# Start-up of a two-layer trunk kernel: x by 256 columns, weights in three cuts, first scaled copies on VectorE

## The chip, the cores and the metric

The kernel runs on one core of one Trainium2 chip. The metric is the device time of one launch in microseconds (us); less is better. One core has TensorE (PE, matrix products; its weight loads are listed as PEld), VectorE (DVE), ScalarE (ACT), GpSimd (POOL) and SyncE (SP, which here issues most transfers). The engines run on their own and wait for each other through semaphores.

## The reference

Two layers (DEPTH = 2) over x of 256 tokens and 1024 columns, all in fp32. What the change touches is the very beginning of layer 0: the norm and the first part of the combined projection.

```python
def rms_norm(x, g):
    xf = x.astype(jnp.float32)
    y = xf * lax.rsqrt(jnp.mean(xf * xf, axis=-1, keepdims=True) + EPS)
    return (y * g.astype(jnp.float32)).astype(x.dtype)

u = rms_norm(h, g_mix_pre)
(gq, gk, gv, gg, ra_f, ra_b, aq, ak, av, gate_a, gate_b) = jnp.split(u @ w_in, offsets, axis=-1)
```

Behind it come gated linear attention, attention with rotary positions, a merge, an output projection, a SwiGLU network and a per-layer embedding, twice.

## The kernel before

Every product is made of three passes. A factor is split into a high part (rounded to the matmul's format, by ACT) and a low part (the remainder, by VectorE); TensorE adds high x high, high x low and low x high. Weights come in units of about 1 MB (class `Stream`): SP issues the load into one of two raw buffers (`rawp`), ACT casts the high part `wh`, VectorE subtracts to get the low part `wl`, TensorE reads both. A raw buffer is free for the next load when its low parts are made; `ws.load()` issues the next load, `ws.pieces()` gives the two halves of a unit (high, low, raw).

The first four units are rows of `w_in`: unit n has k-tiles 2n and 2n + 1 (128 rows each) of 1056 columns: the decay ranks and the queries. The 1056 columns go to TensorE in three blocks `RQ` of 288, 384 and 384 columns, for both halves (`hf`) of 128 tokens, so six accumulators `acc_0rq`.

In layer 0 the row scale of the norm is applied later, so TensorE need not wait for it. The left factor is x transposed, times the gain column. `turn` transposes a 128x128 block of x on TensorE into a PSUM bank (one bank for four k-tiles of one half), `high` makes the scaled high part from it on ACT, `rest` the scaled remainder on VectorE (`scalar_tensor_tensor`, PSUM times gain minus high). `gains` transposes the gain vector into the column `gcol`. `low` makes a weight's low part, `split_here` both parts of a weight.

The order of this phase is written out by hand. `on(e, ...)` chains the instructions of one engine (or of SP's transfers, "dma") in the order in which they are written. The generator `start` emits the work in portions: `yield n` hands back until n ticks have passed, and the matmul loops call `tick()` after each group. The first portion holds the transposes of k-tiles 0 to 3, the scaled copies and the splits of the first unit. Transposes of later k-tiles, the splits of the second unit, the squares for the norm, and the third unit follow in later portions.

Transfers before: x columns 0-511 of half 0 on SP, of half 1 on ACT's queue, then the small gain vector on ACT's queue; k-tiles 0 and 1 of the first unit as two transfers of 1056 columns (`FIRST`); the second unit in one transfer; x columns 512-1023 as two.

Warm-up matmuls on constant data (`warm_up`) run before x is there: `WARM = 6, 6, 3` means six of 128 columns, six of 512, and three of 512 after the first transposes.

The first unit's matmuls (`rq_first`) run k-tile by k-tile over all six accumulators; units 1 to 3 go through `rq_step`, one accumulator and unit at a time, in the order `STEPS_FIRST`.

Of the kernel before, what the change touches and what calls it, by code (L numbers as in the profile page):

```python
# [48 lines left out]
UNIT = 2112  # L49
RQ = ((0, 288), (288, 672), (672, 1056))  # L50

WARM = 6, 6, 3

FIRST = (0, 0, 1056), (1, 0, 1056)
C_GQ, C_GK, C_GV, C_GG, C_RA = 0, 512, 1024, 2048, 3072
C_AQ, C_AK, C_GA, C_GB = 3104, 4128, 4640, 5664

# [2 lines left out]
def trunk_kernel(ctx: ExitStack, tc: tile.TileContext, a: dict, out: bass.AP):  # L60
# [78 lines left out]
    def on(e, f, *args, **kw):  # L139

        with tc.issue_after(line[e].ins) if e in line else nullcontext():
            line[e] = f(*args, **kw)
# [6 lines left out]

    grow = mid()[0:8, 0:P]  # L150

    def load_x(hf, j, e="dma", q=nc.sync):
        c = slice(j * 512, (j + 1) * 512)
        on(e, q.dma_start, h[:, hf, c], a["x"][0, hf * P : (hf + 1) * P, c])

    load_x(0, 0)
    load_x(1, 0, "act", nc.scalar)
    on("act", nc.scalar.dma_start, grow, a["g_mix_pre"][0].rearrange("(k p) -> k p", p=P))


# [29 lines left out]
    def unit_rows(w, n, c0=0, c1=D, parts=None):  # L190

        if parts:

            return lambda t: [
                (t[:, k * (c1 - c0) + x : k * (c1 - c0) + y], w[(2 * n + k) * P : (2 * n + k + 1) * P, c0 + x : c0 + y])
                for k, x, y in parts
            ]
        return lambda t: [
            (
                t[:, : 2 * (c1 - c0)].rearrange("p (k c) -> p k c", k=2),  # L200
                w[n * 256 : (n + 1) * 256, c0:c1].rearrange("(k p) c -> p k c", p=P),
            )
        ]

    plan = []
    for l in range(DEPTH):
        w = a["w_in"][l]
        plan += [unit_rows(w, n, C_RA, C_RA + 1056, FIRST if l + n == 0 else None) for n in range(4)]
        for c0 in (C_AK, C_GQ, C_GK, C_GV, C_GV + 512, C_GG, C_GG + 512):
            plan += [unit(w, kh, c0) for kh in range(2)]  # L210
        by_block = lambda w, c: [unit(w, kh, c + j * 512) for j in range(2) for kh in range(2)]
        gates, merges = by_block(w, C_GA), by_block(a["w_o_gla"][l], 0)
        pair = [unit(w, kh, C_GB + j * 512) for kh in range(2) for j in range(2)]
        for x in GATES:
            plan.append(gates.pop(0) if x == "u" else merges.pop(0) if x == "m" else (pair, int(x)))
        plan += by_block(a["w_o_attn"][l], 0)
        plan += [unit(a["w_out"][l], kh, j * 512) for kh in range(2) for j in range(2)]
        if l == 0:
            plan += [unit_rows(a["w_ple_proj"][l], 0)]
        w = a["w_ffn_in"][l]  # L220
        blocks = [[unit_gate_up(w, kh, b) for kh in range(2)] for b in range(NBLK)]
        plan += blocks[0] + blocks[1]
        plains = [u for b in PLAIN for u in blocks[b]]
        pairs = [[unit(w, kh, c + b * 256) for kh in range(2) for c in (0, HIDDEN)] for b in PAIRS]
        outs = [unit_rows(a["w_ffn_out"][l], n) for n in OUT]
        for x in FFN.replace("p", ""):
            if x == "1":
                pair = pairs.pop(0)
            plan.append(plains.pop(0) if x == "u" else outs.pop(0) if x == "o" else (pair, int(x)))
        plan += outs  # L230
        plan += [unit(a["w_ple_gate"][l], kh, j * 512) for kh in range(2) for j in range(2)]
        if l + 1 < DEPTH:
            plan += [unit_rows(a["w_ple_proj"][l + 1], 0)]

    class Load:
# [5 lines left out]
        def start(self):  # L241
            if self.own:
                self.raw = self.own()
            else:
                self.raw = rawp.tile([P, UNIT], F32, tag="raw", name=nm("raw"))
            return self.make(self.raw)

    class Stream:
# [33 lines left out]
                self.lend = False  # L282
            return wp.tile([P, UNIT], F32R, tag=tag, name=nm("lent")).bitcast(F32)

        def load(self, between=lambda: None):

            self.room += 1
            self.start(between)

        def start(self, between=lambda: None):  # L290
            while self.loads and (self.lend or not self.loads[0].waits) and (self.loads[0].own or self.room):
                x = self.loads.pop(0)
                self.room -= not x.own
                moves = x.start()
                for dst, src in moves:
                    if self.open:
                        nc.sync.dma_start(dst, src)
                    else:
                        on("dma", nc.sync.dma_start, dst, src)
                    between()  # L300
                x.n = sum(math.prod(dst.shape[1:]) for dst, _ in moves)

        def put(self, x, parts=2):
# [476 lines left out]


    ws.load()
    ws.load()
    load_x(0, 1)
    load_x(1, 1)
    unit_a, unit_b = ws.pieces()
    warm = accp.tile([P, 512], F32, tag="acc", name="warm")
    gcol = small(8, "gcol", 1)
# [42 lines left out]
    def gains():  # L831

        ps = aux()
        on("pe", nc.tensor.transpose, ps[:, 0:8], grow, ident[0:8, 0:8])
        on("dve", nc.vector.tensor_copy, gcol, ps[:, 0:8])
# [4 lines left out]
    def split_here(hi, lo, src):  # L840
        on("act", nc.scalar.copy, hi, src)
        low(hi, lo, src)
# [11 lines left out]
    def high(hf, *ks):  # L854

        for k in ks:
            ps = banks[hf, k // 4][:, k % 4 * P : (k % 4 + 1) * P]
            on("act", nc.scalar.activation, uT.at(k, 1, hf * P, P)[0][:, 0, :], ps, AF.Copy, bias=0.0, scale=gcol[:, k : k + 1])

    def rest(hf, *ks):  # L860

        for k in ks:
            ps = banks[hf, k // 4][:, k % 4 * P : (k % 4 + 1) * P]
            hi, lo = (t[:, 0, :] for t in uT.at(k, 1, hf * P, P))
            on("dve", nc.vector.scalar_tensor_tensor, out=lo, in0=ps, scalar=gcol[:, k : k + 1],
               in1=hi.bitcast(F32), op0=ALU.mult, op1=ALU.subtract)

    def start():
        cut = lambda piece, c: [t[:, c] for t in piece]
        gains()  # L870
        for hf in range(2):
            turn(hf, 0)
        for hf in range(2):
            high(hf, 0)
        warm_up(WARM[2], True)
        turn(0, 1)
        turn(1, 1)
        turn(0, 2, 3)
        for c in RQ:
            on("act", nc.scalar.copy, *(t[:, slice(*c)] for t in unit_a[::2]))  # L880
        rest(0, 0)
        rest(1, 0)
        low(*cut(unit_a, slice(0, 288)))
        high(0, 1)
        high(1, 1)
        low(*cut(unit_a, slice(288, 1056)))
        on("act", nc.scalar.copy, unit_b[0], unit_b[2])
        rest(0, 1)
        rest(1, 1)
        high(0, 2, 3)  # L890
        low(*unit_b)
        rest(0, 2, 3)
        ws.load()
        unit_c, unit_d = ws.pieces()
        yield 2
        turn(1, 2, 3)
        high(1, 2, 3)
        rest(1, 2, 3)
        yield 4
        split_here(*unit_c)  # L900
        split_here(*unit_d)
        ws.load()
        for hf in range(2):
            square(hf, 0)
        yield 2
        turn(0, 4, 5, 6, 7)
        for hf in range(2):
            square_here(hf, 1)
            rstd(hf)
        scales()  # L910
        ropes_first.extend(rope_tables(0))
        high(0, 4, 5, 6, 7)
        rest(0, 4, 5, 6, 7)
        yield 1
        turn(1, 4, 5, 6, 7)
        high(1, 4, 5, 6, 7)
        rest(1, 4, 5, 6, 7)
        for piece in ws.pieces():
            split_here(*piece)
        ws.load()  # L920
        ws.open = True
        ws.fill()
# [53 lines left out]
    for l in range(DEPTH):  # L976
# [92 lines left out]
            passes(o[:, : c1 - c0], parts, u == 0, u == 3, u == 0)  # L1069
            tick()  # L1070

        def rq_first(os_):

            for k in range(2):
                for hf, ps in ((0, (0, 2)), (1, (0, 2)), (0, (1,)), (1, (1,))):
                    ah, al = uT.tok(k, hf)
                    for b, (c0, c1) in enumerate(RQ):
                        h, lo = (t[:, k * 1056 + c0 : k * 1056 + c1] for t in us[0])
                        for p in ps:
                            x, y = ((ah, h), (ah, lo), (al, h))[p]  # L1080
                            mm(os_[hf, b][:, : c1 - c0], x, y, k + p == 0, False)
                    tick()

        steps = [(int(x[0]), b, int(x[1])) for x in (STEPS if l else STEPS_FIRST) for b in range(3)]
# [1 line left out]
        for n, (hf, b, u) in enumerate(steps):  # L1086
            if u == len(us):
                us.append(ws.take())
            if (hf, b) not in o:
                o[hf, b] = acc()  # L1090
            if l + u:
                rq_step(o[hf, b], hf, b, u)
            elif (hf, b) == (1, 2):
                rq_first(o)
            if all(s[2] != u for s in steps[n + 1 :]):
                ws.done()
            if u == 3:
                put_q(hf, b, o[hf, b])
# [608 lines left out]
```

## Time and profile before

| | |
|---|---|
| median of 3 runs | 921.12 us (920.63 to 921.78) |
| the profiled execution | 920.53 us, of which 918.8 us span |
| first matmuls of the first unit without a pause | from 7.66 us on |
| transfers | 173.44 MB, mean 189 GB/s |

How to read the rows: times are microseconds from the start of the span unless marked ns. A row of a timeline gives start, length, engine, line and operation, what is written <- what is read, the shape, the count of merged instructions, and in brackets how long the engine had been idle before and who ended that. A row of the chain of waits gives start, length, engine, tile and line. Instructions that go through `on` carry line 142, the warm-ups and the first unit's matmuls line 105, those of the later units line 121. Matmuls overlap: the spacing of their starts is their price, their own length is longer.

### The profile page before, as it was taken

To read this page: it belongs to the slowest core of one execution; us is meant where nothing else is said; L and a number is where in the kernel's file an instruction comes from. 1 tells how busy PE (TensorE), PEld (TensorE's weight loads), DVE (VectorE), ACT (ScalarE), POOL (GpSimd) and SP (SyncE) were. 2 spreads that over 40 slices of the span, in tenths; PEclk is the share of its full clock that TensorE was granted. 3 is DMA by queue.
4 is the path that set the end of the run, shared out by engine and by line. 5 is a ranking of instruction groups with operands and counts; after the bars stand their busy time and mean duration, and the time that the engine had idled before them with its cause. 6 is when DMAs were issued, how large, how long until landed. Compare 5 with 4: busy or idle time off the path is not lost.

```text
span 918.8 us, 12423 instructions
## 1 busy us (share of the span) xinstructions
PE 909.9 (99%) x4673; PEld 776.1 (84%) x4673; DVE 785.2 (85%) x1004; ACT 583.1 (63%) x968; POOL 93.1 (10%) x149
## 2 busy tenths in 40 slices
PE   9999999999999999999999999999999999999996
PEld 8998888888888888888899988888888888888886
DVE  6988989987669998999779789798875799989984
ACT  6688767564567565567675677765644766565563
POOL 3700212310000000000114001100001000000000
PEclk9999999999999999999999999999999999999999
DMA  8664445657385655657576424454673856555361
GB/s 277 206 199 135 138 138 189 212 184 244 107 298 183 210 197 189 244 158 260 195 238 210 158 92 138 138 202 164 201 256 103 278 170 212 215 173 225 124 243 46
DMA packets 88679, 173.44 MB, mean 189 GB/s; under 512 B 3422, under 2 KB 26470, under 8 KB 88108
## 3 DMA queue, kind: packets, MB, share of 16 engines
q1 hardware_dynamic: 88316, 172.27, 55.1%
q8 instruction: 36, 0.59, 0.3%
q10 hardware_dynamic: 304, 0.40, 0.1%
q14 instruction: 23, 0.19, 0.1%
HBM read 169.50 MB, written 3.15 MB: 188 GB/s over the span
## 4 chain that ended last, share of the span: by engine, by line
PE 92%; DVE 4%; issue 1%; ACT 1%; POOL 1%; DMA 1%; POOLq 0%; DVEq 0%; SPq 0%; ACTq 0%
PE acc_1ffnin L121 11%; PE acc_0ffnin L121 11%; PE acc_0gate L121 7%; PE acc_1gate L121 7%; PE acc_1ffnin L105 7%; PE acc_0ffnin L105 6%; PE acc_1rq L121 3%; PE acc_0gqk L121 3%; PE acc_0wout L121 2%; PE acc_1gqk L121 2%; PE acc_0ple L121 2%; PE acc_1gg L121 2%; PE acc_0v L121 2%; PE acc_0merge L121 2%; PE acc_1merge L121 2%; PE acc_1ple L121 2%
## 5 line engine op out<-in xcount | busy, mean ns | idle before, releaser
L105 PE MATMUL acc_0ffnin<-wh_0ffnin,big_0ffnin 128*128 128x512 f32 x176 | 57.0, 393 | 0.1
L105 PE MATMUL acc_1ffnin<-wh_1ffnin,big_1ffnin 128*128 128x512 f32 x176 | 56.8, 392 | 0.0
L133 ACT CAST wh_1ffnin<-raw_1ffnin 128x1024 fp32r<-128x1024 f32 x38 | 38.5, 1049 | 27.1 <-DMA raw_1ffnin<-in_w_ffn_out_dram 8.6
L133 ACT CAST wh_0ffnin<-raw_0ffnin 128x1024 fp32r<-128x1024 f32 x38 | 38.2, 1048 | 24.9 <-PE acc_0ffnin L121 7.4
L133 DVE TENSOR_TENSOR wl_1ffnin<-raw_1ffnin,wh_1ffnin 128x1024 fp32r<-128x1024 f32 x38 | 45.0, 1223 | 8.8 <-ACT wh_1ffnin L133 8.7
L133 DVE TENSOR_TENSOR wl_0ffnin<-raw_0ffnin,wh_0ffnin 128x1024 fp32r<-128x1024 f32 x38 | 44.7, 1222 | 8.1 <-ACT wh_0ffnin L133 8.0
L121 PE MATMUL acc_0ffnin<-wh_0ffnin,big_0wout 128*128 128x512 f32 x168 | 42.5, 393 | 0.0
L121 PE MATMUL acc_1ffnin<-wh_1ffnin,big_1wout 128*128 128x512 f32 x168 | 42.5, 393 | 0.0
L105 PEld LDWEIGHTS acc_0ffnin<-wh_0ffnin,big_0ffnin 128*128 128x128 f32 x176 | 33.0, 188 | 7.2 <-DVE big_0ffnin L133 0.5
L105 PEld LDWEIGHTS acc_1ffnin<-wh_1ffnin,big_1ffnin 128*128 128x128 f32 x176 | 33.0, 188 | 6.7
L133 DVE TENSOR_TENSOR wl_1ffnin<-lent_1ffnin,wh_1ffnin 128x1024 fp32r<-128x1024 f32 x30 | 35.9, 1221 | 1.7 <-ACT wh_1ffnin L133 1.7
L133 DVE TENSOR_TENSOR wl_0ffnin<-lent_0ffnin,wh_0ffnin 128x1024 fp32r<-128x1024 f32 x30 | 35.9, 1221 | 1.7 <-ACT wh_0ffnin L133 1.7
L121 PEld LDWEIGHTS acc_1ffnin<-wh_1ffnin,big_1wout 128*128 128x128 f32 x168 | 31.1, 188 | 6.2
L121 PEld LDWEIGHTS acc_0ffnin<-wh_0ffnin,big_0wout 128*128 128x128 f32 x168 | 31.1, 188 | 6.2
L133 ACT CAST wh_1ffnin<-lent_1ffnin 128x1024 fp32r<-128x1024 f32 x30 | 30.7, 1052 | 7.3 <-PE acc_1ffnin L105 3.9
L133 ACT CAST wh_0ffnin<-lent_0ffnin 128x1024 fp32r<-128x1024 f32 x30 | 30.7, 1054 | 7.0 <-PE acc_0ffnin L105 3.9
L105 PE MATMUL acc_1ffnin<-wl_1ffnin,big_1ffnin 128*128 128x512 f32 x88 | 34.3, 390 | 0.0
L105 PE MATMUL acc_0ffnin<-wl_0ffnin,big_0ffnin 128*128 128x512 f32 x88 | 34.3, 390 | 0.0
L133 DVE TENSOR_TENSOR wl_0gate<-raw_0gate,wh_0gate 128x1024 fp32r<-128x1024 f32 x20 | 24.3, 1260 | 5.3 <-ACT wh_0gate L133 5.2
L133 ACT CAST wh_0gate<-raw_0gate 128x1024 fp32r<-128x1024 f32 x20 | 20.0, 1049 | 13.1 <-DMA raw_0gate<-in_w_o_attn_dram 6.3
L133 DVE TENSOR_TENSOR wl_1gate<-raw_1gate,wh_1gate 128x1024 fp32r<-128x1024 f32 x20 | 23.6, 1223 | 5.4 <-ACT wh_1gate L133 5.2
L133 ACT CAST wh_1gate<-raw_1gate 128x1024 fp32r<-128x1024 f32 x20 | 20.0, 1049 | 11.7 <-DMA raw_1gate<-in_w_o_attn_dram 5.7
(710 smaller groups left out, 2705.4 us busy)
## 6 DMA issues: line engine op xcount, KB each, us to landing
raw_0ffnin<-in_w_ffn_out_dram SPq DMA_DIRECT2D x11, 1024.0 KB, 5.6
raw_1ffnin<-in_w_ffn_out_dram SPq DMA_DIRECT2D x11, 1024.0 KB, 5.2
lent_0ffnin<-in_w_ffn_in_dram SPq DMA_DIRECT2D x6, 1024.0 KB, 7.7
lent_1ffnin<-in_w_ffn_in_dram SPq DMA_DIRECT2D x6, 1024.0 KB, 6.7
raw_0v<-in_w_in_dram SPq DMA_DIRECT2D x4, 1024.0 KB, 4.9
raw_0gate<-in_w_o_gla_dram SPq DMA_DIRECT2D x4, 1024.0 KB, 5.2
raw_0gate<-in_w_o_attn_dram SPq DMA_DIRECT2D x4, 1024.0 KB, 5.6
raw_0wout<-in_w_ffn_in_dram SPq DMA_DIRECT2D x8, 512.0 KB, 5.0
```

The costliest lines, as they stand in the source:

```text
L105: return nc.tensor.matmul(o, lhsT, rhs, start=start, stop=stop)
L121: nc.tensor.matmul(o, x, y, start=start and n == 0, stop=stop and n == len(seq) - 1, **kw)
L133: return nc.scalar.copy(hi, src), nc.vector.tensor_tensor(out=lo, in0=src, in1=hi.bitcast(F32), op=ALU.subtract)
```

## The change

The first transfers, all on SP: x columns 0-255 of all 256 tokens; k-tile 0 as 288 and 768 columns, k-tile 1 as 1056; x columns 256-511; the second unit as two transfers of 1056 columns; x columns 512-1023. ACT's queue keeps the gain vector alone. Warm-ups become six narrow and three wide, and two narrow after the transposes. The first scaled copies of k-tiles 0 and 1, four in all, move from ACT to VectorE (`high_here`). The transposes of k-tile 1 come right behind those of k-tile 0; k-tiles 2 and 3 are turned in later portions. The cast of k-tile 1's weights on ACT is cut into the three blocks, its low part into two. `rq_first` now does the first two units, each k-tile by k-tile; in k-tile 0 it goes block by block over both halves, otherwise half by half.

```diff
-WARM = 6, 6, 3
+WARM = 6, 3, 2
-FIRST = (0, 0, 1056), (1, 0, 1056)
+FIRST = ((0, 0, 288), (0, 288, 1056), (1, 0, 1056)), ((0, 0, 1056), (1, 0, 1056))
...
-    def load_x(hf, j, e="dma", q=nc.sync):
-        c = slice(j * 512, (j + 1) * 512)
-        on(e, q.dma_start, h[:, hf, c], a["x"][0, hf * P : (hf + 1) * P, c])
-    load_x(0, 0)
-    load_x(1, 0, "act", nc.scalar)
+    def load_x(c0, c1):
+        on("dma", nc.sync.dma_start, h[:, :, c0:c1], a["x"][0, :, c0:c1].rearrange("(s p) c -> p s c", p=P))
+    load_x(0, 256)
...
     ws.load()
+    load_x(256, 512)
     ws.load()
-    load_x(0, 1)
-    load_x(1, 1)
+    load_x(512, 1024)
...
+    def high_here(hf, k):
+        ps = banks[hf, k // 4][:, k % 4 * P : (k % 4 + 1) * P]
+        hi = uT.at(k, 1, hf * P, P)[0][:, 0, :]
+        on("dve", nc.vector.tensor_scalar, out=hi, in0=ps, scalar1=gcol[:, k : k + 1], scalar2=None, op0=ALU.mult)
...
     def start():
+        def split_cut(piece):
+            for c in RQ:
+                on("act", nc.scalar.copy, *(t[:, slice(*c)] for t in piece[::2]))
         gains()
-        for hf in range(2):
-            turn(hf, 0)
-        for hf in range(2):
-            high(hf, 0)
-        warm_up(WARM[2], True)
-        turn(0, 1)
-        turn(1, 1)
-        turn(0, 2, 3)
-        for c in RQ:
-            on("act", nc.scalar.copy, *(t[:, slice(*c)] for t in unit_a[::2]))
+        for k in range(2):
+            for hf in range(2):
+                turn(hf, k)
+        warm_up(WARM[2])
+        for hf in range(2):
+            high_here(hf, 0)
+        split_cut(unit_a)
         rest(0, 0)
         rest(1, 0)
         low(*cut(unit_a, slice(0, 288)))
-        high(0, 1)
-        high(1, 1)
+        for hf in range(2):
+            high_here(hf, 1)
         low(*cut(unit_a, slice(288, 1056)))
-        on("act", nc.scalar.copy, unit_b[0], unit_b[2])
+        split_cut(unit_b)
         rest(0, 1)
         rest(1, 1)
-        high(0, 2, 3)
-        low(*unit_b)
-        rest(0, 2, 3)
+        low(*cut(unit_b, slice(0, 288)))
+        low(*cut(unit_b, slice(288, 1056)))
         ws.load()
         unit_c, unit_d = ws.pieces()
-        yield 2
+        yield 5
+        turn(0, 2, 3)
+        high(0, 2, 3)
+        rest(0, 2, 3)
+        split_here(*unit_c)
+        yield 1
         turn(1, 2, 3)
         high(1, 2, 3)
         rest(1, 2, 3)
-        yield 4
-        split_here(*unit_c)
+        yield 2
         split_here(*unit_d)
         ws.load()
         for hf in range(2):
             square(hf, 0)
-        yield 2
+        yield 3
         turn(0, 4, 5, 6, 7)
...
-        def rq_first(os_):
+        def rq_first(os_, u):
+            both = (0, 1)
             for k in range(2):
-                for hf, ps in ((0, (0, 2)), (1, (0, 2)), (0, (1,)), (1, (1,))):
-                    ah, al = uT.tok(k, hf)
-                    for b, (c0, c1) in enumerate(RQ):
-                        h, lo = (t[:, k * 1056 + c0 : k * 1056 + c1] for t in us[0])
-                        for p in ps:
-                            x, y = ((ah, h), (ah, lo), (al, h))[p]
-                            mm(os_[hf, b][:, : c1 - c0], x, y, k + p == 0, False)
+                rows = [[(b, hf, p) for p in (0, 2) for hf in both] for b in range(3)] if u + k == 0 else [
+                    [(b, hf, p) for b in range(3) for p in (0, 2)] for hf in both
+                ]
+                for row in rows + [[(b, hf, 1) for b in range(3)] for hf in both]:
+                    for b, hf, p in row:
+                        ah, al = uT.tok(2 * u + k, hf)
+                        c0, c1 = RQ[b]
+                        h, lo = (t[:, k * 1056 + c0 : k * 1056 + c1] for t in us[u])
+                        x, y = ((ah, h), (ah, lo), (al, h))[p]
+                        args = os_[hf, b][:, : c1 - c0], x, y, u + k + p == 0, False
+                        if u + k == 0 and p != 1:
+                            on("pe", mm, *args)
+                        else:
+                            mm(*args)
                     tick()
...
-            if l + u:
+            if l or u > 1:
                 rq_step(o[hf, b], hf, b, u)
             elif (hf, b) == (1, 2):
-                rq_first(o)
+                rq_first(o, u)
```

More of the change, by code (lines that the diff above doesn't have):

```diff
@@ L207, in trunk_kernel @@
         w = a["w_in"][l]
-        plan += [unit_rows(w, n, C_RA, C_RA + 1056, FIRST if l + n == 0 else None) for n in range(4)]
+        plan += [unit_rows(w, n, C_RA, C_RA + 1056, FIRST[n] if l == 0 and n < 2 else None) for n in range(4)]
         for c0 in (C_AK, C_GQ, C_GK, C_GV, C_GV + 512, C_GG, C_GG + 512):
@@ L283, in lent, with load, start @@
             return wp.tile([P, UNIT], F32R, tag=tag, name=nm("lent")).bitcast(F32)
-        def load(self, between=lambda: None):
+        def load(self):
             self.room += 1
-            self.start(between)
-        def start(self, between=lambda: None):
+            self.start()
+        def start(self):
             while self.loads and (self.lend or not self.loads[0].waits) and (self.loads[0].own or self.room):
@@ L299, in start @@
                         on("dma", nc.sync.dma_start, dst, src)
-                    between()
                 x.n = sum(math.prod(dst.shape[1:]) for dst, _ in moves)
```

## The prediction

> **What bounds the kernel now.** I read the page first, then the chain of waits in order of time, then the timeline of each engine over the first 36 us.
>
> ```profile
> PE 909.9 (99%) x4673; PEld 776.1 (84%) x4673; DVE 785.2 (85%) x1004; ACT 583.1 (63%) x968; POOL 93.1 (10%) x149
> ...
> PE 92%; DVE 4%; issue 1%; ACT 1%; POOL 1%; DMA 1%; POOLq 0%; DVEq 0%; SPq 0%; ACTq 0%
> ```
>
> TensorE (PE) is busy 909.9 of 918.8 us and carries 92% of the chain. What the change can win is the time at the start in which TensorE does nothing useful; whatever it wins there survives only if no later unit of weights is missed. The chain of waits (start, length, what):
>
> ```profile
> 1.04 3.38 PE warm L105 x12
> 4.42 0.12 issue
> 4.54 0.86 PE aux_start L142 x3
> 5.40 1.28 PE warm L105 x3
> 6.68 0.47 PE aux_start L142 x4
> ...
> 7.26 0.36 DVE big_start L142
> 7.62 0.04 issue
> 7.66 2.51 PE acc_0rq L105 x14
> 10.18 0.22 PE aux_start L142 x2
> 10.39 3.08 PE acc_0rq L105 x19
> 13.48 0.44 PE aux_start L142 x4
> ...
> 32.02 5.23 PE acc_0kv L121 x23
> ```
>
> Until 7.66 us the chain is warm-up matmuls, transposes and one wait for VectorE (DVE). The first unit (36 matmuls, k-tiles 0 and 1; some records are missing) ends at 13.48. Nineteen of its matmuls take 3.08 us, so 0.162 us each. From 13.48 on TensorE has no gap in the first 36 us.
>
> The pace matters. Three 512-column warm-ups take 1.28 us, 0.427 each; 512-column matmuls later take 5.23/23 = 0.227. So until about 6.6 us TensorE runs at half pace, though the granted clock (the last column but two of this stage row) reads 1.00 there:
>
> ```profile
> 5.75:6.00 0.25, 0.25 (x2) 0.02 (x1) 0.00 (x0) 0.24 (x2) 0.00 (x0) 1.00 0.94 389
> ```
>
> At half pace a column costs 0.427/512 us: 288 columns 0.24 us, 384 columns 0.32. The four transposes from 6.68 (0.47 us for four, against 0.86 for three before) are already at full pace. I go by the spacing, not by the granted clock.
>
> **The change: transfers.** Bytes moved, per microsecond from 0 on (view of the transfers, first 40 us), and the landings of the first x:
>
> ```profile
> GB/s 0 23 260 411 372 384 418 406 411 380 282 31 144 384 427 290 181 350 363 350 174 125 220 397 383 12 4 127 401 403 113 35 170 406 401 53 0 16 59 209
> h<-in_x_dram ACTq DMA_DIRECT2D x1, 256.0 KB, 3.4
> h<-in_x_dram SPq DMA_DIRECT2D x1, 256.0 KB, 3.2
> 0.79 0.38 SPq L142 DMA_DIRECT2D h<-in_x_dram  x1
> 1.22 1.38 SPq L142 DMA_DIRECT2D raw_start<-in_w_in_dram  x3
> ```
>
> Summed, the row gives 283 kB by 3.0 us, 694 by 4.0, 1066 by 5.0, 1450 by 6.0, 1868 by 7.0. The 524 kB of x are through at 3.6 and land at 4.0 and 4.2 (issue 0.79 + 3.2, and 3.4 on ACT's queue): 0.4 to 0.6 us after the last byte; I take 0.45. The new order is 262 kB of x, 147 kB and 393 kB of k-tile 0, 541 kB of k-tile 1, x columns 256-511, k-tiles 2 and 3, the rest of x. On the same curve these land at 3.35, 3.8, 4.8, 6.2, 6.9, 8.2, 9.5 and 10.9. [...] SP issues eight transfers at 0.46 (1.38/3) instead of six, done by 4.5, and only the load of g_gla_out stands behind them; ACT issues one fewer. That costs nothing: the next load that SP issues waits for VectorE anyhow (10.82, below).
>
> **Warm-up and transposes.** [...] The gain column's transpose needs only its own small load, now alone on ACT's queue. Four transposes from 3.35 at about 0.21 us issue spacing: half 0 has both k-tiles at 4.25, half 1 at 4.5. The three wide warm-ups that stood on the chain at 5.40 (1.28) become two narrow ones of 0.21, under VectorE's copies.
>
> **First scaled copies on VectorE.** No such copy of 128x128 from PSUM on VectorE is in the trace; the nearest rows:
>
> ```profile
> 5.22 0.63 ACT L142 ACTIVATE big_start<-aux_start,gcol_start 128x128 fp32r<-128x128 f32 x2 [2.10 <-PE aux_start L142]
> 5.86 1.26 ACT L142 CAST wh_start<-raw_start 128x288 fp32r<-128x288 f32 x3
> ...
> 7.26 0.61 DVE L142 SCALAR_TENSOR_TENSOR big_start<-aux_start,gcol_start,big_start 128x128 fp32r<-128x128 f32 x2 [2.27 <-PE aux_start L142]
> 7.79 1.32 DVE L142 TENSOR_TENSOR wl_start<-raw_start,wh_start 128x288 fp32r<-128x288 f32 x2
> ...
> 9.54 1.25 DVE L142 TENSOR_TENSOR wl_start<-raw_start,wh_start 128x1056 fp32r<-128x1056 f32 x1
> ```
>
> Two remainders take 0.61, so 0.27 spacing and 0.34 length; I use the same for a scaled copy (bounds 0.17, the 128x8 copy that VectorE makes at 4.82, and 0.37, ACT's length).
>
> ```profile
> 4.82 0.17 DVE L142 COPY gcol_start<-aux_start 128x8 f32<-128x8 f32 x1 [3.23 <-PE aux_start L142]
> ```
>
> The remainder at 7.26 waited 2.27 us for transposes, although its own k-tile had been turned at 5.2: it waits for whatever was written to that bank before it. That's why I let the copies wait for both k-tiles. Copies run 4.35-4.95, remainders of k-tile 0 until 5.5. ACT is free to cast: 288 columns by 4.25, the two others by 5.3 and 5.75 (a third of the 1.26 row each, some 0.45).
>
> **TensorE in the new order.** First matmul at 4.75. The four of block 0 are paced by VectorE (copy, copy, remainder, remainder) to 5.8. Then two at 0.32 until about 6.5, and at full pace six of 384 columns at 0.17: 7.5. Six with the weights' low part, 0.97: 8.5 (VectorE has those low parts at 7.3: two more copies 0.54, low parts 1.32). Two transposes, 0.22: 8.7. Eighteen matmuls of k-tile 1 at 0.162 and two more transposes: 8.7 + 2.9 + 0.22 = 11.8. Before: 13.48. **Lead 1.7 us.**
>
> [...]
>
> **Does the lead hold?** The second unit needs its high part from ACT at 10.5 and 12.1 (casts of 1.03, half of the 2.05 row below, behind the scaled copies), TensorE reaches it at 11.8 and 14.7. The tight one is the third:
>
> ```profile
> 10.82 0.38 SPq L142 DMA_DIRECT2D raw_start<-in_w_in_dram  x1
> 16.74 2.05 ACT L142 CAST wh_start<-raw_start 128x1056 fp32r<-128x1056 f32 x2 [0.41 <-DMA raw_start<-in_w_in_dram]
> 17.86 2.43 DVE L142 TENSOR_TENSOR wl_start<-raw_start,wh_start 128x1056 fp32r<-128x1056 f32 x2
> 20.54 0.29 PE L121 MATMUL acc_0rq<-wl_start,big_start 128*128 128x288 f32 x1
> 21.19 0.29 PE L121 MATMUL acc_0rq<-wl_start,big_start 128*128 128x288 f32 x1
> ```
>
> Its second low part is ready at 20.29 and first read at 21.19: slack 0.9. VectorE is busy from 7.26 to 20.29 without a pause but 0.23: 12.8 us of work. The change adds four copies (4 x 0.27 = 1.1) and one cut more in a low part (1.32 for two against 1.25: 0.1), and starts at 4.35. I add 0.7 of pauses: VectorE waits for ACT, which casts k-tile 2 only after two scaled copies that wait for TensorE's transposes at 8.5. 4.35 + 12.8 + 1.2 + 0.7 = 19.1. TensorE would read at 21.19 - 1.7 = 19.5, so the lead just holds, with 0.4 to spare; beyond that each tenth on VectorE costs a tenth. The third unit's load goes out when the first unit's raw buffer is free, at about 9.1 instead of 10.82; with the 5.9 us from 10.82 to 16.74 it lands at 15.0, before ACT is through with its copies (near 15.9). ACT has four copies less (2 x 0.63 = 1.26) and one cast cut in three (1.26 for 1.07 in one piece).
>
> The sum goes against the profiled execution: 920.53 us with a span of 918.8, the rest outside the span and untouched. 920.53 - 1.7 = 918.8; the median of the runs shown is 921.12, 0.6 above that execution, so the forecast for it is **919.4**. The cover that can go: VectorE's margin of 0.4 (1.3 us of extra delay there would leave 0.8 of the 1.7).
>
> **Rivals.** [...]
> (b) VectorE's backlog: 2.0 us of pauses instead of 0.7, low parts of the third unit at 20.4, TensorE stalls 0.9: gain 0.8, 920.3. For it: 12.8 us without a pause. Against: the next load is freed earlier too.
> [...]
> [...]
> That the change doesn't do what it says: x lands at 4.2 as now. Then everything up to 8.5 moves by 0.85, and the gain is 0.9; it falls in with (b) at 920.2.
>
> **How the numbers follow.** Forecast 0.40, (a) 0.10, (b) with the late x 0.12, (c) 0.25, (d) 0.13. A measurement of this kernel can tell 0.2%, 1.84 us, from no change: faster means under 919.28, slower over 922.96. The forecast's own range is 918.8 to 920.0 (x landing 3.0 to 3.6, copies 0.17 to 0.37), and the bound at 919.28 lies in its middle: half of it, 0.20, is faster, half the same. Faster: 0.20 + 0.25 = 0.45. Same: 0.20 + 0.10 + 0.12 = 0.42. Slower: 0.13. The range 918.3 to 921.5 takes in (a), (b) and most of (c) and leaves out (d) and the far end of (c).
>
> **What would show it.** In the changed profile: first x-transposes near 3.4; VectorE's scaled copies near 4.4 with 0.27 spacing; first acc_0rq matmul near 4.75; 0.32 us between 384-column matmuls turning to 0.17 near 6.6; the last matmul of the first unit near 11.8; low parts of the third unit by 19.1 and read at 19.5. Wrong it is if half pace goes on beyond 7 us, if TensorE waits for VectorE at the third unit, or if x lands no earlier than 4.

## The result, and the profile after

The changed kernel takes 922.64 us (median of 17 runs, 921.63 to 923.93), the kernel before 920.90 beside it (17 runs, 920.12 to 921.78). The ratio is 1.0020, 95% interval 1.0013 to 1.0027: 1.7 us slower. The profiled execution took 922.96 us (span 921.2) against 920.53 (918.8) before.

The page's first rows, with the chain's shares by engine:

```profile
PE 911.5 (99%) x4669; PEld 778.3 (84%) x4669; DVE 786.2 (85%) x1009; ACT 581.4 (63%) x966; POOL 92.7 (10%) x149
...
PE 94%; DVE 2%; ACT 1%; DMA 1%; issue 1%; POOL 1%; SPq 0%; POOLq 0%; DVEq 0%; ACTq 0%
```

TensorE was busy 911.5 us instead of 909.9, although it has six wide warm-ups fewer and only two narrow ones more: of the 2.4 us of span, 1.6 is TensorE being busy longer, and 0.8 is idle time. So two things went wrong. The chain of waits of the changed kernel (start, length, what) shows both:

```profile
1.79 4.60 DMA raw_start<-in_w_in_dram
...
6.42 0.52 ACT wh_start L142
...
6.98 4.69 PE acc_0rq L105 x14
...
12.09 1.23 PE acc_0rq L105 x6
...
13.54 3.84 PE acc_0rq L105 x24
...
22.11 11.62 PE acc_0rq L121 x72
...
33.95 5.23 PE acc_0kv L121 x23
```

First, a transfer now opens the chain: k-tile 0's second piece, issued at 1.79, lands at 6.39, and TensorE goes on only at 6.98. Second, fourteen matmuls from there take 4.69 us, 0.335 each: half pace. Only near 12.1 to 13.5 does the spacing become 0.16 (3.84/24). The trace's own record of TensorE's clock has its first change, to full, at 12.54; in the kernel before it was at 6.58. The keys and values start at 33.95 instead of 32.02, 1.93 late. From 6.98 on TensorE doesn't pause in this stretch.

TensorE's timeline has the pause (last column: idle before, and who ended it):

```profile
3.58 1.11 PE L142 MATMUL aux_start<-ident,h 128*128 128x128 f32 x4 [0.23 <-DMA h<-in_x_dram]
4.49 0.42 PE L105 MATMUL warm<-seed 128*128 128x128 bf16 x2
5.01 1.30 PE L105 MATMUL acc_0rq<-wh_start,big_start 128*128 128x288 f32 x4
6.98 2.93 PE L105 MATMUL acc_0rq<-wh_start,big_start 128*128 128x384 f32 x8 [0.67 <-ACT wh_start L142]
```

VectorE's timeline, the first scaled copies and the third unit's low parts:

```profile
4.52 0.61 DVE L142 TENSOR_SCALAR big_start<-aux_start,gcol_start 128x128 fp32r<-128x128 f32 x2 [0.97 <-PE aux_start L142]
...
21.11 2.42 DVE L142 TENSOR_TENSOR wl_start<-raw_start,wh_start 128x1056 fp32r<-128x1056 f32 x2
```

And ScalarE's, its first casts and the third unit's:

```profile
3.92 0.43 ACT L142 CAST wh_start<-raw_start 128x288 fp32r<-128x288 f32 x1 [1.20 <-DMA raw_start<-in_w_in_dram]
6.42 0.92 ACT L142 CAST wh_start<-raw_start 128x384 fp32r<-128x384 f32 x2 [2.06 <-DMA raw_start<-in_w_in_dram]
...
19.87 2.10 ACT L142 CAST wh_start<-raw_start 128x1056 fp32r<-128x1056 f32 x2
```

ACT sat idle 2.06 us for the second piece. VectorE's copies came as forecast, 4.52 and a spacing of 0.27 (0.61 for two). The third unit's cast, at 16.74 before, is at 19.87. It costs nothing here, because TensorE at half pace is late too. The third unit's load itself (its issue, then its landing in the view of the transfers) took 7.9 us, so it landed near 18.0; before, it was 5.9 us from issue to cast.

```profile
10.11 0.38 SPq L142 DMA_DIRECT2D raw_start<-in_w_in_dram  x1
...
raw_start<-in_w_in_dram SPq DMA_DIRECT2D x1, 1056.0 KB, 7.9
```

The view of the transfers, first 40 us: bytes moved per microsecond, and landings of the two pieces (the last column is the time from issue):

```profile
GB/s 0 17 284 189 326 358 320 324 403 415 392 338 227 351 326 203 121 88 161 401 406 329 135 14 53 207 408 377 23 129 399 414 96 45 227 403 365 16 0 0
...
raw_start<-in_w_in_dram SPq DMA_DIRECT2D x1, 384.0 KB, 4.6
...
raw_start<-in_w_in_dram SPq DMA_DIRECT2D x1, 144.0 KB, 2.6
```

Up to 3 us it moved as much as before (301 against 283 kB). From 3 to 4 it moved 189 instead of 411. The view by stages gives the next four microseconds (window, its length, granted clock, share of time that the DMA engines are busy, GB/s), first before:

```profile
4.00:8.00 4.00, 1.00 1.01 395
```

then after:

```profile
4.00:8.00 4.00, 1.00 0.99 332
```

The DMA engines are as busy and move 16% less. By 8.0 us 0.45 MB are missing (1.82 MB of 2.27).

### The profile page after: what moved, and what is told of

Read it like the earlier page. It is cut to its first block, busy times and chain, and to the rows that moved or that the text cites. A ratio compares the mean times of both kernels' runs of the same rounds, so it can differ in the third digit from the quotient of the medians.

```text
span 921.2 us, 12422 instructions
## 1 busy us (share of the span) xinstructions
PE 911.5 (99%) x4669; PEld 778.3 (84%) x4669; DVE 786.2 (85%) x1009; ACT 581.4 (63%) x966; POOL 92.7 (10%) x149
## 4 chain that ended last, share of the span: by engine, by line
PE 94%; DVE 2%; ACT 1%; DMA 1%; issue 1%; POOL 1%; SPq 0%; POOLq 0%; DVEq 0%; ACTq 0%
PE acc_0ffnin L121 12%; PE acc_1ffnin L121 11%; PE acc_1gate L121 7%; PE acc_0gate L121 7%; PE acc_0ffnin L105 7%; PE acc_1ffnin L105 7%; PE acc_1rq L121 3%; PE acc_0gqk L121 2%; PE acc_0wout L121 2%; PE acc_1gqk L121 2%; PE acc_0ple L121 2%; PE acc_1gg L121 2%; PE acc_0v L121 2%; PE acc_1merge L121 2%; PE acc_0merge L121 2%; PE acc_1ple L121 2%
## 5 line engine op out<-in xcount | busy, mean ns | idle before, releaser
L133 ACT CAST wh_1gate<-raw_1gate 128x1024 fp32r<-128x1024 f32 x20 | 20.1, 1050 | 12.1 <-DMA raw_1gate<-in_w_o_attn_dram 5.7
```

The source lines that it names most:

```text
L133: return nc.scalar.copy(hi, src), nc.vector.tensor_tensor(out=lo, in0=src, in1=hi.bitcast(F32), op=ALU.subtract)
```

## The experiments

Two theories from here on. CLOCK: a pause on TensorE ahead of full pace puts full pace off (in after a pause of 0.67 us ended at 6.98, and the clock was up at 12.54; in before the longest was 0.12, and it was up at 6.58); fewer warm-ups and the wait for the second piece make such pauses. TRANSFERS: the cut of k-tile 0 on SP's queue slows the first transfers, so that its second piece and the third unit are late. "Clock up" below is the first change in the trace's clock record, the spacing of matmuls agrees with it. "Reached" is the start of the first keys-and-values matmuls' stretch in the chain, 32.02 before and 33.95 after. The last four columns are of one profiled execution each, the median is of all runs.

| kernel | median us (lowest to highest) | before beside it | ratio, 95% | clock up | k-tile 0 complete | GB/s 4 to 8 us | reached |
|---|---|---|---|---|---|---|---|
| before (profile) | | | | 6.58 | | 395 | 32.02 |
| after (profile) | 922.64 (921.63–923.93) | 920.90 | 1.0013–1.0027 | 12.54 | 6.39 | 332 | 33.95 |
| e10, after again | 921.92, one run | 920.78 | | 7.85 | 6.07 | 284 | 32.75 |
| e1, after, filled | 922.00 (921.05–922.51) | 920.79 | 1.0002–1.0019 | 4.72 | 6.77 | 310 | 33.12 |
| e8, after, warm-ups of before | 921.46 (920.44–923.09) | 920.78 | 0.9996–1.0013 | 5.14 | 6.47 | 327 | 32.78 |
| e3, after, k-tile 0 whole | 921.67 (919.69–922.82) | 920.79 | 1.0001–1.0018 | 9.94 | 5.84 | 377 | 32.97 |
| e6, e3 filled | 921.34 (920.08–922.81) | 920.70 | 0.9996–1.0013 | 6.84 | 5.30 | 375 | 31.52 |
| e4, after, second piece on ACT's queue | 921.89 (921.47–925.09) | 920.79 | 1.0007–1.0026 | 10.46 | 5.3 | 382 | 32.80 |
| e5, e4 filled | 920.89 (919.38–922.89) | 920.70 | 0.9993–1.0010 | 5.50 | 5.4 | 395 | 30.95 |
| e12, e4 filled densely | 920.79 (919.63–922.31) | 920.66 | 0.9990–1.0009 | 5.87 | 5.4 | 352 | 30.93 |
| e7, after, loads and warm-ups of before | 920.63 (919.80–921.52) | 920.70 | 0.9991–1.0008 | 3.90 | 6.02 | 409 | 31.57 |
| e9, x on ACT's queue | 923.08 (922.12–924.46) | 920.78 | 1.0013–1.0034 | 9.87 | 5.12 | 395 | 33.45 |
| e2, before, fewer warm-ups | 921.90 (920.95–923.00) | 920.79 | 1.0000–1.0018 | 8.47 | | 379 | 32.54 |
| e11, before, k-tile 0 cut | 921.03 (920.29–922.46) | 920.66 | 0.9995–1.0013 | 5.23 | 6.97 | 332 | 32.67 |

### Fill TensorE's pauses (e1)

```diff
-WARM = 6, 3, 2
+WARM = 6, 4, 1
-        warm_up(WARM[2])
+        warm_up(WARM[2], True)
...
+                    if u + k + b == 0 and p == 2:
+                        for _ in range(2):
+                            on("pe", mm, os_[1, 2], seed, keep, True, True)
```

Two matmuls on constants go behind the fourth matmul; the accumulator that they write starts anew later.

> The changed kernel with its pauses on TensorE filled: one wide warm-up more before x, one wide in place of two narrow after the transposes, and two 512-column matmuls on constant data (into an accumulator that is cleared afterwards) between the first four and the fifth matmul. Theory CLOCK (the change lost because a pause of 0.67 us before the fifth matmul put full pace off from 6.6 to 12.5 us): full pace by 7.9 us at the latest, first unit done by 13.0 instead of 17.0 or so for the same work, time 919.8 to 920.6, 2 us below the changed kernel. Theory TRANSFER (the loss is the wait for the weights and the waits of ACT and VectorE behind it): the pause only holds other work, time 922.4 to 923.0 as the changed kernel.

The clock came up at 4.72, as CLOCK asks, and the median was 922.0 all the same, between the range that CLOCK gave and the one of TRANSFERS. The time went to another place; TensorE at the third unit in this run:

```profile
20.31 0.53 PE L121 MATMUL acc_0rq<-wh_start,big_start 128*128 128x288 f32 x2 [0.30 <-ACT wh_start L142]
21.28 0.89 PE L121 MATMUL acc_0rq<-wh_start,big_start 128*128 128x288 f32 x4 [0.44 <-ACT wh_start L142]
```

and the chain there:

```profile
2.25 6.12 DMA raw_start<-in_w_in_dram
...
9.69 0.97 DVE wl_start L142
...
10.68 8.48 DMA raw_start<-in_w_in_dram
...
19.18 0.88 ACT wh_start L142
...
20.16 1.07 ACT wh_start L142
...
21.28 11.63 PE acc_0rq L121 x70
```

The chain never touches TensorE before 21.28: k-tile 1's landing at 8.37 sets when the raw buffer comes free, hence the third unit's load at 10.68, which needs 8.5 us (before: 5.9 from issue to cast). A clock nearly 8 us earlier than in the profile of after won 0.83 us at the keys and values (33.95 to 33.12). The two costs stand in for each other: whoever removes one meets the other.

### Fewer warm-ups alone, in the kernel before (e2)

```diff
-WARM = 6, 6, 3
+WARM = 6, 3, 3
```

> The kernel before with three wide warm-ups fewer at the start, nothing else. They end at 3.1 instead of 4.4 us, x lands at 4.0 to 4.2: a pause of about 1 us. [...] Theory TRANSFER: 920.7 to 921.0, no change, because the warm-ups stand in a wait for x.

```profile
4.45 0.24 PE L142 MATMUL aux_start<-ident,mid_start 8*128 8x8 f32 x1 [1.30 <-DMA mid_start<-in_g_mix_pre_dram]
```

That is TensorE's timeline of e2: three warm-ups less leave a pause of 1.30 us; the clock comes up at 8.47 and the median rises by 1.1 us (the interval just touches no difference). In the profile of before they cover that wait, and the clock is up at 6.58.

### K-tile 0 whole again (e3), and whole and filled (e6)

```diff
-FIRST = ((0, 0, 288), (0, 288, 1056), (1, 0, 1056)), ((0, 0, 1056), (1, 0, 1056))
+FIRST = ((0, 0, 1056), (1, 0, 1056)), ((0, 0, 1056), (1, 0, 1056))
```

e6 has `WARM = 6, 4, 4` besides, the last four wide.

> The changed kernel with k-tile 0 as one transfer of 1056 columns again. If the cut made the transfer slow (third transfer starts at 245 GB/s and less between 3 and 4.2 us): k-tile 0 lands near 5.2 as a whole, first matmul at 5.7, no pause after it. Theory CLOCK: a pause from 4.7 to 5.7 in place of two of 0.35 and 0.67, dense from 5.7 on; full pace between 7 and 9.1, time 920.0 to 921.5. Theory TRANSFER: the weights arrive 1.2 us earlier, time 921.3 to 921.6, at whatever pace.

> k-tile 0 in one transfer as in the third experiment, TensorE kept busy until the first matmul (one wide warm-up more before x, four wide after the transposes). The third had its first matmul at 6.34 and half pace until 9.94. Theory CLOCK AND TRANSFER: full pace by 7.9 us, first matmul at 6.4, first unit done near 12.4, 919.8 to 920.5. Rival SUPPLY: 920.7 to 921.4, with a wait at the third unit. If CLOCK is no cause: 921.7 as the third.

The view by stages of e3:

```profile
4.00:8.00 4.00, 1.00 1.01 377
```

The whole k-tile of 528 KB is there at 5.84, before the last 384 KB of the cut one (6.39), and the rate is back. But TensorE now waits for its first matmul, and the clock comes at 9.94. Its timeline:

```profile
6.34 3.81 PE L105 MATMUL acc_0rq<-wh_start,big_start 128*128 128x288 f32 x12 [1.04 <-ACT wh_start L142]
```

Its median, 921.67, is above both ranges expected. With the pauses filled (e6) the clock is at 6.84 and the keys and values are reached 0.50 us ahead of before; its median is nevertheless 0.6 above before, an interval that includes no difference, and above the 919.8 to 920.5 of CLOCK AND TRANSFER. It lies in the range of the rival SUPPLY, but the wait at the third unit that this rival asks for isn't in the profile.

### The second piece on ACT's queue (e4), and filled (e5, e12)

```diff
-                for dst, src in moves:
-                    if self.open:
+                for i, (dst, src) in enumerate(moves):
+                    if i == 1 and len(moves) == 3:
+                        on("act", nc.scalar.dma_start, dst, src)
+                    elif self.open:
...
```

e5 has `WARM = 6, 4, 3` and e12 `WARM = 6, 5, 2` besides, the last ones wide.

> The changed kernel with the 768-column transfer of k-tile 0 issued by ACT instead of SP, so issued 0.5 us earlier and on the other queue. If the late landing (6.4 us) comes from the start of each small transfer behind the one before on a single queue: it lands near 5.2, the pause before the fifth matmul is gone. Theory CLOCK: full pace by 8 us in most runs, 920.0 to 921.0. Theory TRANSFER: 1.2 us less than the changed kernel, 921.4. If it still lands after 6, both expect 922.4 to 923.

> The 768 columns on ACT's queue as in the fourth experiment, and TensorE kept busy until the first matmul: one wide warm-up more before x, three wide in place of two narrow after the transposes. The fourth experiment began its first unit at 5.58 us but ran at half pace until 10.46. Theory CLOCK AND TRANSFER (both were needed): full pace by 7.9 us at the latest, first matmul at 5.8, first unit done near 12, 919.3 to 920.0, so 0.8 to 1.5 below the kernel before. Rival SUPPLY (the third unit's load, landing after 18 us, is the next bound, as in the first experiment where TensorE waited for its cast at 20.3 and 21.3): full pace early, but a wait of 1 us and more at the third unit, 920.5 to 921.3. If CLOCK is no cause: 921.9 as the fourth.

> The variant of the fifth experiment (768 columns on ACT's queue, TensorE kept busy) with one wide warm-up moved from behind the transposes to ahead of them: six narrow, five wide, two wide. [...] Theory CLOCK: full pace by 7.9 us in every execution, the slow executions (921.5 to 922.9) go, median 919.8 to 920.5 against 920.9. If the spread of the fifth had another cause (transfers): median and spread as there.

With the same cut on two queues the rate is 382 and both pieces are there at 5.3, the second 1.1 sooner than in after; but the first, which now shares the time with it, lands at 5.07 (3.8 us after its issue). So TensorE's timeline of e4 has its pause before the first matmul:

```profile
5.58 3.89 PE L105 MATMUL acc_0rq<-wh_start,big_start 128*128 128x288 f32 x12 [0.70 <-ACT wh_start L142]
```

With this one pause full pace came at 10.46 only: the pause has moved, not gone, and the median misses both theories' figures. e5 fills it, and its chain runs over TensorE alone from the transposes on:

```profile
0.79 3.23 DMA h<-in_x_dram
...
4.07 1.11 PE aux_start L142 x4
5.18 0.87 PE warm L105 x3
6.05 2.99 PE acc_0rq L105 x18
...
19.04 11.69 PE acc_0rq L121 x72
```

Eighteen matmuls take 2.99 us (0.166 each), the third unit is read from 19.04 on without a wait, and this execution took 919.45 us: it keeps its lead of 1.07 at the keys and values to the end. This is the course that the prediction described, some 1 us later and with the transfers split over two queues. Its twelve executions spread over 3.5 us, though, and their median of 920.89 is no better than before. e12, with one warm-up moved ahead of the transposes, reaches the keys and values 1.09 ahead too; in its profile most of that is lost at the start of layer 1, where TensorE waits in its timeline:

```profile
471.63 1.32 PE L446 MATMUL aux_0ple<-ident,mid_0ple 128*128 128x128 f32 x8 [0.40 <-DVE mid_0ple L516]
```

The profile of before has no such wait there. At the first keys and values of layer 1 0.35 of e12's lead is left (494.54 against 494.89). Its chain of waits there comes over a load of weights, ACT and VectorE, and reaches TensorE late:

```profile
459.55 6.39 DMA raw_0ple<-in_w_in_dram
...
472.63 2.43 DVE wl_1emb L133 x2
...
475.71 6.33 PE acc_1rq L121 x38
```

The chain of e6 does the same (a load of 6.04 us from 460.85 on, TensorE only from 476.67); e6, already 0.17 behind before at 444.55, is 0.61 behind at 495.50. In the profiles of before and e5 the chain stays on TensorE there. The spread of e12, expected to be narrower, stayed at 2.7 us, its median missed the 919.8 to 920.5 of CLOCK, and why some executions lose the lead later is open.

The medians, each less that of the before beside it, say the same: after +1.7; with the clock alone mended (e1, and e8 below) +1.2 and +0.7; with the transfers alone mended (e3, e4) +0.9 and +1.1; with both (e5, e12) +0.2 and +0.1, and +0.6 in e6.

### The new order with the loads of before (e7); the warm-ups of before with the new loads (e8)

e7 takes `FIRST`, `load_x` and its calls from before, and `WARM = 6, 6, 3`; e8 only `WARM = 6, 6, 3`. In both the last three are wide.

> The changed order of the work (copies on VectorE, two units k-tile by k-tile, later transposes) with the transfers and warm-ups of the kernel before (x by 512 columns on two queues, k-tiles 0 and 1 and the second unit uncut, six narrow, six wide, three wide). Only transfers and warm-ups are undone. If the loss came from these alone: full pace near 6.6, first matmul near 6.8 without the wait for remainders at 7.3, 920.0 to 920.8, at or below the kernel before. If the new order itself costs (VectorE's 1.2 us of extra work, ACT waiting for late transposes): 921.3 to 922.

> The changed kernel with the warm-ups of the kernel before (six narrow, six wide, three wide), nothing else undone. The transposes then start at 4.4 instead of 3.6 us and the first matmul at 6.6 instead of 5.0, but TensorE has hardly a pause. Theory CLOCK: full pace by 7.9 at the latest, first unit done near 13, 921.0 to 921.8, about 1.2 below the changed kernel, though its first matmul is 1.6 us later. If CLOCK is no cause, the later start only costs: 923 to 924.

e7 equals before (ratio 1.0000) and reaches the keys and values 0.45 us ahead, with a clock that in this profile came up 2.7 us earlier (3.90): the copies on VectorE and the k-tile order of two units cost nothing, and gain no more than that. e8 differs from e7 in the loads alone, and is 1.2 us behind it there; in its view by stages and on TensorE:

```profile
4.00:8.00 4.00, 1.00 0.95 327
```

```profile
19.98 0.53 PE L121 MATMUL acc_0rq<-wh_start,big_start 128*128 128x288 f32 x2 [0.27 <-ACT wh_start L142]
20.95 0.88 PE L121 MATMUL acc_0rq<-wh_start,big_start 128*128 128x288 f32 x4 [0.44 <-ACT wh_start L142]
```

The new loads, with a clock at 5.14, give the wait at the third unit again. The median, 921.46, is in CLOCK's range.

### X on ACT's queue (e9)

```diff
-    load_x(0, 256)
+    load_x(0, 256, "act", nc.scalar)
```

K-tile 0 whole on SP, `WARM = 6, 6, 1` with the last one wide.

> The changed kernel with the first 256 columns of x on ACT's queue beside k-tile 0 in one piece on SP's, and warm-ups six narrow, six wide, one wide. Both transfers are issued at 0.8 us. If a small transfer alone on a queue was what let the weights come late: k-tile 0 lands at 4.8 to 5.2 instead of 6.4, x at 4.0 to 4.2, first matmul at 5.6, full pace by 7.9, 919.5 to 920.5, below the kernel before. If the weights are late for another reason (they land after 5.8): 920.7 to 921.5, no better than the one-piece variant.

K-tile 0 is there at 5.12, as expected, but the time is a miss, by a queue that I had not counted: the gain vector now stands behind x on ACT's queue.

```profile
5.65 0.24 PE L142 MATMUL aux_start<-ident,mid_start 8*128 8x8 f32 x1 [1.22 <-DMA mid_start<-in_g_mix_pre_dram]
```

4 KB land at 5.5, TensorE's timeline has a pause of 1.22, the clock is at 9.87, and it is the slowest of all.

### The changed kernel again (e10), and the cut alone in the kernel before (e11)

e10 has no edit. e11:

```diff
-FIRST = (0, 0, 1056), (1, 0, 1056)
+FIRST = (0, 0, 288), (0, 288, 1056), (1, 0, 1056)
```

> The changed kernel itself once more, for a second profile of it. [...] If the late clock was an accident of one execution: full pace near 6.6.

> The kernel before with one part of the change alone: k-tile 0 as 288 and 768 columns on SP's queue. In all four profiles with this cut behind the first x on that queue the transfers moved 284 to 332 GB/s between 4 and 8 us, in all eight without it 375 to 409. Theory CUT (the cut itself slows the transfers): 335 GB/s or less between 4 and 8 us, the third unit's cast later than 16.74 us, 921.2 to 922.0. Rival FIRST X (it takes the short first x, after which the cut pieces start with nothing moving; here x by 512 columns on two queues covers their start): 375 GB/s and more, no change, 920.5 to 921.0.

The same program in another execution (e10) had its clock up at 7.85, neither at 12.54 again nor near 6.6, and its pause of 0.68 stood ahead of the transposes, not ahead of the fifth matmul. It waited at the third unit instead; its chain there:

```profile
12.96 6.60 DMA mid_start<-in_w_alpha_up_dram
...
19.58 0.04 ACTq L774
...
19.78 1.08 ACT wh_start L142
...
20.90 11.63 PE acc_0rq L121 x70
```

Here the third unit's second cast stands on ACT behind a wait of line 774 for small loads that SP issued behind the third unit's and that took 6.6 us to land. ACT's timeline shows that the third unit's own load held up the first cast, and that the second follows without a pause:

```profile
18.80 2.05 ACT L142 CAST wh_start<-raw_start 128x1056 fp32r<-128x1056 f32 x2 [1.04 <-DMA raw_start<-in_w_in_dram]
```

Two casts took 2.05 before as well, so the small loads cost nothing beyond the late third unit.

e11 shows the transfers' part by itself, with every other line as before. View by stages, then TensorE's timeline:

```profile
4.00:8.00 4.00, 1.00 0.99 332
```

```profile
7.56 2.30 PE L105 MATMUL acc_0rq<-wh_start,big_start 128*128 128x384 f32 x11 [0.96 <-ACT wh_start L142]
```

One cut on SP's queue gives the rate of after, 332, and a pause of 0.96 us behind the first matmul. At the keys and values that is 0.65 late, though the clock was up sooner than in the profile of before (5.23). The third unit's cast is at 18.11 instead of 16.74, as the theory CUT of this run asks. The median rises by 0.37, less than expected, and the interval includes no difference.

## Why the prediction was wrong

The forecast was 919.4 with a range up to 921.5; it was 922.64. Rival (d), with 0.13, was the one above that range. In the profile of after the pause ahead of the fifth matmul came from a transfer, by way of ACT, and not from VectorE, and TensorE did not wait at the third unit.

- **Landing of x, copies: right.** Transposes start at 3.58 (forecast 3.35), the copies on VectorE at 4.52 with 0.27 spacing (4.35), the first matmul at 5.01 (4.75). No run shows the 3.0 at which the forecast's range begins: where the transposes waited for x (after, e3, e4, e5, e10), they started at 3.56 to 4.07.
- **Transfers: wrong.** The step "on the same curve these land at 3.35, 3.8, 4.8" took the old curve for new transfers. K-tile 0's second piece landed at 6.39, not 4.8, and the first near 3.9 as forecast. On the curve as measured, its last byte (802 kB in all) would have passed at 5.0 and landed at 5.4: 0.6 of the 1.6 us is the lower rate. The other 1.0 the curve doesn't hold, because it takes the bytes in the order of issue. The packet records of the trace show otherwise: the last of the piece's 128 packets (3072 bytes each) ended at 6.05, and by then 78 packets of 4224 bytes, 0.33 MB, of transfers issued later had ended. The landing followed 0.34 behind the last packet, so it took no longer than the 0.45 of the forecast. The range allowed for a late x alone; the pieces had none. e11 shows the cut alone to bring 332 GB/s, and e4 the same cut on two queues to bring 382 (e5 395, e12 352).
- **Full pace near 6.6: wrong.** I kept the old kernel's 6.6 although the change takes 1.28 us of cover away. It came at 12.54, and at 7.85 in e10. In after TensorE had pauses of 0.23, 0.11 and 0.67 us ahead of it, in e10 one of 0.68, where before has one of 0.12 ahead of 6.58. Rivals (a) and (d), the two with a later clock, together had 0.23; that before came to full pace only after 5.5 us of nearly unbroken work (1.04 to 6.58) spoke for more. Rival (c), 0.25, had an earlier clock, which neither profile of the changed kernel shows.
- **Third unit: wrong, and hidden.** "It lands at 15.0" took an issue at 9.1 and the old 5.9 us. In the profile of after the issue was at 10.11 and the landing 7.9 us later, near 18.0; the cast begins at 19.87, behind scaled copies on ACT that wait for transposes at 17.38, and costs nothing only because TensorE is at half pace. In e1, e8 and e10, with the clock up earlier, TensorE waits there 0.44 to 0.74 us.

The sum with the measured terms: the fifth matmul starts at 6.98 where the forecast had 5.8, 1.18. From 6.98 to 12.54 TensorE runs 5.56 us at half pace, of which half, 2.78, is loss; the forecast had already paid about 0.3 of it for two matmuls. -1.7 + 1.18 + 2.48 = +1.96, measured +1.93 at the keys and values. Another 0.5 comes in later in that execution and isn't traced to a cause.

What the runs don't settle: why cutting k-tile 0 on one queue lowers the rate, and why leads of 0.5 to 1.1 us at 32 us (e6, e5, e12) often don't reach the end. So the gain of 1.7 us itself, in the median, was reached by no run.

## What to carry to other kernels

A start that is bound by its transfers must be costed with the transfers of the new order, not with the old rate curve: a cut of a first load on the same queue lowered the rate in all five profiles that have it (284 to 332 GB/s), while the same cut over two queues gave 352 to 395, against 375 to 409 without a cut. Before taking away warm-up matmuls that seem to cover nothing, look for the pauses that appear and how long each is: in e2 three fewer left a pause of 1.30 us, and the clock was up at 8.47 instead of 6.58. And where two late things run side by side, mending one only shows the other: e1 still has the late transfers, e4 the pause, and e5 has neither, and only comes level with the kernel before.

## What the runs showed of the hardware

- **When the clock comes up.** In the trace's clock record the first change, to full, is at 12.54 us in the profile of after and at 7.85 in e10, the same program. Where TensorE had no pause over 0.30 us between its first matmul and that change (before, e1, e5 to e8, e11, e12; 0.30 in e5), it came at 3.90 to 6.84; where it had one of 0.67 (after), 0.68 (e10), 0.70 (e4) or 1.04 to 1.30 (e3, e9, e2), at 7.85 to 12.54. The pauses of e1 (0.68) and e11 (0.96) came when the clock was up, and full pace went on behind them: eight matmuls in 1.68 us in e1 and eleven in 2.30 in e11, against eight in 2.93 in after at half pace. The length of the longest pause alone doesn't set the time: 0.67 and 0.68 go with 12.54 and 7.85. The time between the clock's two changes was 907.945 us in the profile of before, 904.532 in that of after and 911.359 in that of e7; these differ by 3.413 and 3.414. What the clock counts the runs don't show. The granted clock of the stage rows reads 1.00 ahead of the first change, at half pace too (4.00 to 8.00 us in after, with 0.335 us a matmul from 6.98 on).
- **Cut transfers.** 144 and 384 KB in place of 528 KB on SP's queue: 284 to 332 GB/s from 4 to 8 us in after, e1, e8, e10 and e11, against 375 to 409 in before, e2, e3, e6, e7 and e9, with the DMA engines busy 0.90 to 1.03 of the time in both. With the second piece on ACT's queue (e4, e5, e12) it was 382, 395 and 352. The third unit's load, issued after 9.6 us, took 7.4 to 8.6 us with the cut on SP's queue, 5.4 to 6.1 without a cut and 6.1 to 7.3 over two queues.
- **Packets of later transfers go ahead.** In after 0.33 MB of transfers issued later had passed on the same queue before the last packet of k-tile 0's second piece ended, at 6.05.
- **A small load behind a large one.** The 4 KB gain vector landed at 5.51 behind 256 KB of x on ACT's queue in e9, and at 4.32 and 4.53 in e2 and e7; alone on it, it was there for its transpose at 3.08 (e10, e4).
